# Gate logits copied out of their bank by VectorE alone, and the second half's norm factors spread by a store and a load

## Chip, cores and metric

One core of a Trainium2 chip runs the kernel. The metric is the device time of one execution in microseconds (us). The kernel before was timed in three runs; the profile shown below is of a fourth execution of the same program.

## What is computed

One layer of a decoder trunk on x of 1024 rows by 1024 columns in float32, cut here to what the change touches:

```python
h    = rms_norm(x, norm_mix_g)                  # r = (mean(x*x) + eps) ** -0.5 for each row, h = x * r * g
proj = h @ w_in                                 # q k v z_a gk_low cb cc xc z_c g_a g_c
gk   = log_sigmoid(gk_low @ w_gk2 + b_gk) / 16  # the decays, 4 heads of 128
o    = gla_chunked(q, k, v, gk)                 # uses running sums of gk in chunks of 64 rows
...
```

What is left out is the convolution branch, the gated merge, the output product, the gate of the per-layer embedding and the last norm.

## The kernel before

Everything is held transposed: columns of x on the 128 partitions, rows along the free dimension. The rows come in two halves of 512. Each large product is split into quadrants and computed by a scheme of seven products per 2x2 block (h0 to h6 are the seven combinations of h's quadrants), and each float32 operand is split into a rounded part (`hi`, made by ScalarE) and a rest (`lo`, made by VectorE), so that one product costs three matmuls (`mm3`).

The order of instructions is not the order of the program text. `Flow.note` (L270) records each operation with a cost and a latency; `set_dues` (L373) gives each a due time, counted back from the end; `put_in_order` (L420) then deals them out to the five engines' queues, one at a time: each engine takes, of the operations that are ready at the earliest moment, the one with the earliest due time. A `hurry` makes an operation due earlier by so many us. TensorE's main products (`nc.side = False`) keep the order of the text; its side products are fitted in between. `since` (L433) says from when an operation may run, by the inputs and by the release of its buffer. The queues that come out are fixed: on the chip each engine waits at the head of its queue for whatever is late.

Two places matter here.

**The norm factors, `scale_h` (L1083).** It is called for the first half of the rows (i = 0) and for the second (i = 1). For the second half ScalarE squares and sums four row blocks `xn` (128x1024), VectorE adds eps, GpSimd takes the power -0.5, which leaves `r` as 128 partitions by 4. But h needs r along the free dimension, the same on all partitions. So VectorE copies r out to `rb` (128x512), TensorE transposes four 128x128 blocks of it into a PSUM bank `rt`, and VectorE multiplies eight times: `hq <- hq * gain * rt`. From the scaled quarters `hq` VectorE and ScalarE make h1, h2, h4, h5, h6 (`step`, L1139). h0 and h3 come from the first half alone, and the eight gate products of this stage (`two_products`) use only these two.

**The decays, `decays` (L1305).** Woven into the products for v (half 0) and for z_a (half 1), a first product gives `lowp`, which is split into `low`; then for each of the four heads one matmul `zp` of 128x512 goes into a PSUM bank with the tag "o". Two such banks exist, and the main products hold one or the other of them for part of the time. The bank `zp` is read twice: ScalarE takes |zp + b| out of it into `t1`, VectorE takes min(zp + b, 0) into `c`. Exp, Ln, a subtraction and a scan along the rows follow, and a store. The pool "v" (L1273), which holds these tiles and the weights `glw` of `lowp`, takes over the memory of the pool "prep0" with the quarters `hq`.

Of the kernel before, what the change touches and what calls it, by code (L numbers as in the profile page):

```python
# [9 lines left out]
F32 = mybir.dt.float32  # L10
# [3 lines left out]
AF = mybir.ActivationFunctionType  # L14
ALU = mybir.AluOpType

P = 128
# [27 lines left out]
PE, DVE, ACT, POOL, SP = range(5)  # L45
# [197 lines left out]

class Op:
    __slots__ = ("n", "engine", "call", "args", "kw", "cost", "lat", "side", "table", "bytes", "name",
                 "preds", "succs", "left", "ready", "due", "start", "bufs", "hurry")


class Port:
# [7 lines left out]
class Flow:  # L257
# [4 lines left out]

    def __init__(self, tc):
        nc = tc.nc
        self.tc, self.ops, self.side, self.open, self.hurry, self.bundle, self.hold = tc, [], True, [], 0.0, None, None
        self.tensor, self.vector, self.scalar = Port(self, PE, nc.tensor), Port(self, DVE, nc.vector), Port(self, ACT, nc.scalar)
        self.gpsimd, self.sync = Port(self, POOL, nc.gpsimd), Port(self, SP, nc.sync)


    def note(self, engine, op, call, args, kw):  # L270
        views = [a for a in args if isinstance(a, View) or hasattr(a, "ap")]
        views += [a for k, a in kw.items() if k not in ("out", "accum_out") and (isinstance(a, View) or hasattr(a, "ap"))]
        outs, ins = ([kw["out"]], views) if "out" in kw else (views[:1], views[1:])
        if kw.get("accum_out") is not None:
            outs.append(kw["accum_out"])
        o = Op()
        o.n, o.engine, o.call, o.args, o.kw = len(self.ops), engine, call, args, kw
        o.side, o.table, o.bytes, o.bufs, o.hurry = self.side, 0, 0, [], self.hurry
        label = lambda v: v.buf.name if isinstance(v, View) else "in"
        o.name = f"{label(outs[0])}<-{','.join(label(v) for v in ins)}"  # L280
        shape = outs[0].shape
        n = 1
        for d in shape[1:]:
            n *= d
        o.lat = 0.15
        if engine == PE:
            o.cost, o.lat = n / 2400 + 0.0134, 0.22
            if op == "transpose" or args[1].dtype == F32:
                o.cost = 0.11
            elif args[1].shape[0] < P:  # L290
                o.cost = 0.42
        elif engine == DVE:
            psum = any(isinstance(v, View) and v.buf.pool.name == "ps" for v in outs + ins)
            o.cost = 0.07 + n * (0.00055 if op in ("tensor_scalar", "tensor_copy") and not psum else 0.00104)
            if op in ("scalar_tensor_tensor", "tensor_scalar"):
                o.cost += 0.06
            if op == "tensor_tensor_scan":
                o.cost = 0.05 + n * 0.0021
        elif engine == ACT:
            o.cost = 0.10 + n * 0.000833 + (0.2 if "accum_out" in kw else 0.0)  # L300
            o.table = TABLE.get(args[2] if len(args) > 2 else None, 0)
        elif engine == POOL:
            o.cost = 0.1 + n * 0.001 if op == "memset" else 0.6
        else:
            o.cost, o.bytes = 0.4, shape[0] * n * 4
            if getattr(ins[0], "apart", None):
                o.cost, o.bytes = 0.6, 1.4 * o.bytes
            o.lat = 2.0 + o.bytes / 250e3
        if op == "dma_start" and engine != SP:
            o.cost, o.lat = 0.1, 2.3 + shape[0] * n * 4 / 250e3  # L310
        preds = {}

        def behind(p):
            if p is not None and p != o.n:
                q = self.ops[p]
                lat = q.lat
                if q.engine == engine and engine != SP:
                    lat = 0.0 if engine == PE else 0.08
                preds[p] = max(preds.get(p, 0.0), lat)

        for v in ins:
            if isinstance(v, View):
                for b in v.blocks():
                    e = v.buf.memory.setdefault(b, [None, []])
                    behind(e[0])
                    e[1].append(o.n)
        for v in outs:
            if isinstance(v, View):
                for b in v.blocks():
                    e = v.buf.memory.setdefault(b, [None, []])  # L330
                    for p in [e[0]] + e[1]:
                        behind(p)
                    e[0], e[1] = o.n, []
                if engine == PE:
                    behind(v.buf.group)
                    v.buf.group = o.n
                for pool in v.buf.pool.instead:
                    for old in pool.buffers:
                        for p in old.users:
                            behind(p)  # L340
        for v in outs + ins:
            if isinstance(v, View) and v.buf not in o.bufs:
                if v.buf.index is None:
                    v.buf.index = len(v.buf.tag.buffers)
                    v.buf.tag.buffers.append(v.buf)
                o.bufs.append(v.buf)
                v.buf.users.append(o.n)
        if self.hold is not None:
            preds[self.hold] = max(preds.get(self.hold, 0.0), 0.0 if self.ops[self.hold].engine == engine else 0.08)
        o.preds, o.succs = preds, []  # L350
        for p in preds:
            self.ops[p].succs.append(o.n)
        self.ops.append(o)
        if self.bundle is not None and engine == PE:
            self.bundle.append(o)
# [64 lines left out]
    def put_in_order(self):  # L420
# [12 lines left out]
        def since(o):  # L433

            t = max(o.ready, pipe - BACKLOG) if o.engine == SP else o.ready
            for b in o.bufs:
                for e, end in b.ends.items():
                    if e != o.engine:
                        t = max(t, end + 0.13)
                if b.place is None:  # L440
                    if b.tag.next != b.index:
                        return None
                    free = min((w for w in b.tag.free if w is not None), default=None)
                    if free is None:
                        return None
                    t = max(t, free)
            return t

        while len(order) < len(ops):
# [17 lines left out]
            o = ops[n]  # L467
# [11 lines left out]
            for s in o.succs:  # L479
                q = ops[s]  # L480
# [38 lines left out]
def kernel(  # L519
# [16 lines left out]
    nc = Flow(tc)  # L536
# [29 lines left out]
    bgk = vec[:, 0:4]  # L566
# [8 lines left out]
    def dram(name, *shape):  # L575
        return dr.tile([P, *shape], F32, name=name)

    ped = [dram(f"ped{b}", D) for b in range(8)]
    s1d = [dram(f"s1d{c}", 512) for c in range(8)]
    cd = [[dram(f"cd{h}_{i}", HALF) for i in range(2)] for h in range(H)]  # L580
# [22 lines left out]
    def mm(*a, **kw):  # L603
        nc.tensor.matmul(*a, skip_group_check=True, **kw)

    def transpose(o, i):
        nc.tensor.transpose(o, i, ident)
# [433 lines left out]
    with phase("prep0") as pool:  # L1041
# [41 lines left out]
        def scale_h(i):  # L1083
# [3 lines left out]
            r = sm.tile([P, 4], F32, tag="rx", name=f"r_x{i}", bufs=2)  # L1087
            if i:
                ms = sm.tile([P, 4], F32, tag="rn", name="rn")
                for s in range(4):  # L1090
                    act(xn[s], xn[s], AF.Square, scale=1.0 / 32.0, accum_out=ms[:, s:s + 1])
                nc.vector.tensor_scalar(r, ms, EPS, None, op0=ALU.add)
            else:
                acc = slot(1, "h", "sq", (4, 512), F32)
# [8 lines left out]
                    mm(sums[:, s, 0:1], acc[:, 0, s * P:(s + 1) * P], ones, start=True, stop=True)  # L1103
                nc.vector.tensor_scalar(r, sums[:, :, 0], EPS, None, op0=ALU.add)
            nc.gpsimd.tensor_tensor(r, r, mhalf[:, 0:1].to_broadcast([P, 4]), op=ALU.pow)
            rb = bp.tile([P, 4, P], F32, tag="u2", name=f"rb{i}", bufs=2)
            nc.vector.tensor_copy(rb, r[:, :, None].to_broadcast([P, 4, P]))
            rt = pso.tile([P, 4, P], F32, tag="o", name=f"rt{i}", bufs=2)
            for s in range(4):
                transpose(rt[:, s, :], rb[:, s, :])  # L1110
            rt = rt.rearrange("p s t -> p (s t)")
            for n in both:
                for k in range(4):
                    kk = 4 * quad[n][1] + k
# [24 lines left out]
        def step(k):  # L1139
            steps[k]()  # L1140
            hres[k] = hb[k]
# [22 lines left out]
        pe_blocks(range(4, 8), 1)  # L1164
        scale_h(0)
        step(0)
        step(3)
        two_products(pre[:4], (4, 5, 0, 1))
        scale_h(1)
# [103 lines left out]
    with phase("v", [ph["prep0"]]) as qp:  # L1273
# [31 lines left out]
        def decays(half):  # L1305
# [15 lines left out]
            for hp in range(2):  # L1321
                t1 = [qp.tile([P, HALF], F32, tag="t1", name=f"t1_{half}{hp}{i}", bufs=3) for i in range(2)]
                c = [qp.tile([P, HALF], F32, tag="c4", name=f"c4_{half}{hp}{i}", bufs=4) for i in range(2)]
                for i in range(2):
                    h = 2 * hp + i
                    zp = pso.tile([P, 512], F32, tag="o", name=f"zp{half}_{h}", bufs=2)
                    cs = slice(h * P, (h + 1) * P)
                    mm(zp, g2[:, cs], low, start=True, stop=True)
                    act(t1[i], zp, AF.Abs, bias=bgk[:, h:h + 1])
                    nc.vector.tensor_scalar(c[i], zp, bgk[:, h:h + 1], 0.0, op0=ALU.add, op1=ALU.min)  # L1330
                    yield 1
                for t in t1:
                    act(t, t, AF.Exp, scale=-1.0)
# [666 lines left out]
```

## Time and profile before

| | |
|---|---|
| runs | 1078.73, 1078.83, 1078.86 us (median 1078.83) |
| profiled execution | 1078.6 us, of which the span from first to last instruction is 1076.8 us |
| TensorE (PE) busy | 1067.4 us, 99% of the span |
| weight loads (PEld) busy | 892.2 us, 83% |
| VectorE (DVE) busy | 894.3 us, 83% |
| ScalarE (ACT) busy | 623.4 us, 58% |
| GpSimd (POOL) busy | 45.7 us, 4% |
| granted TensorE clock | 0.998 |

Each row of the timeline is a start, a duration, an engine, the operation, the tiles as out<-in, the shape, and in brackets the idle time before it with what ended it. The chain of waits is the list of work that ended last, followed back from the end; its pieces are start, length and what ran. Nearly all lines carry L507, the line at which the planner issues everything, so that one goes by the names of the tiles.

### The profile page before, as it was taken

The page shows a single profiled execution, that of the slowest core. Times are in us where ns is not written, and L with a number is a line of the kernel's source. Part 1 is how long each engine was busy: PE and PEld are TensorE (multiplying, and loading weights), DVE is VectorE, ACT ScalarE, POOL GpSimd, SP SyncE. Part 2 cuts the span into 40 slices and gives each one's busy share as a digit, 9 for nine tenths or more (in the row PEclk, how much of TensorE's full clock was granted, in tenths as well). Part 3 has the DMA queues.
Part 4 walks back from the last instruction along what each step waited for, and adds up shares of the span by engine and source line. Part 5 has one row for each costly group of instructions (what it writes and reads, how often), then busy time and mean ns, then how long its engine had stood idle before and what let it go on. Part 6 is the DMA issues. An engine that isn't in the chain of part 4 may idle for free.

```text
span 1076.8 us, 15006 instructions
## 1 busy us (share of the span) xinstructions
PE 1067.4 (99%) x4989; PEld 892.2 (83%) x4989; DVE 894.3 (83%) x1409; ACT 623.4 (58%) x1141; POOL 45.7 (4%) x83
## 2 busy tenths in 40 slices
PE   9999999999999999999999999999999999999997
PEld 7887887888888888888888888888888888888886
DVE  6998567678999787978868788887999978889896
ACT  6778538656544443555444367666756635466555
POOL 0000000000000000000000011120000000011021
PEclk9999999999999999999999999999999999999999
DMA  9963564467772454554324679978586878799963
GB/s 318 368 229 105 175 209 141 152 196 234 237 222 99 140 183 166 196 194 168 127 85 126 228 238 335 325 277 332 194 305 213 286 223 305 237 337 333 313 222 140
DMA packets 144830, 239.98 MB, mean 223 GB/s; under 512 B 12016, under 2 KB 57328, under 8 KB 141808
## 3 DMA queue, kind: packets, MB, share of 16 engines
q1 hardware_dynamic: 144608, 238.76, 65.5%
q8 instruction: 39, 0.64, 0.2%
q14 instruction: 39, 0.32, 0.1%
q10 hardware_dynamic: 144, 0.26, 0.1%
HBM read 158.24 MB, written 80.74 MB: 222 GB/s over the span
## 4 chain that ended last, share of the span: by engine, by line
PE 98%; ACT 1%; DVE 0%; issue 0%; POOL 0%; ACTq 0%; DVEq 0%
PE vY L507 3%; PE zaY L507 3%; PE pe L507 2%; PE vX L507 2%; PE zaV L507 2%; PE vV L507 2%; PE op L507 2%; PE zaX L507 2%; PE kv L507 1%; PE ga1Y L507 1%; PE ga3Y L507 1%; PE xc1Y L507 1%; PE xc3Y L507 1%; PE cb2Y L507 1%; PE cb1Y L507 1%; PE xc2Y L507 1%
## 5 line engine op out<-in xcount | busy, mean ns | idle before, releaser
L507 ACT ACT_TABLE_LOAD x20 | 25.7, 1283 | 1.1 <-PEq L1989 0.7
L507 ACT ACTIVATE junk<-x 128x512 bf16<-128x512 f32 (+1 forms) x30 | 18.0, 601 | 12.2 <-DVE x L507 9.7
L507 DVE TENSOR_TENSOR wt<-wt 128x512 f32<-128x512 f32 x32 | 22.1, 691 | 0.6 <-DMA wt<-in_wb_dram 0.5
L507 DVE SCALAR_TENSOR_TENSOR u<-t,vec,u 128x1024 f32<-128x1024 f32 x16 | 20.3, 1285 | 0.1
L507 POOL MEMSET t<- 128x2 f32 x8 | 0.8, 100 | 443.2 <-PE k1Y L507 243.0
L507 POOL TENSOR_SCALAR rg<-ms 128x1 f32<-128x1 f32 x8 | 6.4, 796 | 262.5 <-ACT junk L507 262.3
L507 DVE SCALAR_TENSOR_TENSOR S<-S,dds,kv 128x256 f32<-128x256 f32 x24 | 10.5, 478 | 5.4 <-PE kv L507 5.4
L507 ACT CAST S<-S 128x512 fp32r<-128x512 f32 x14 | 8.7, 620 | 10.3 <-PE op L507 9.4
L507 ACT ACTIVATE junk<-op 128x256 bf16<-128x256 f32 x32 | 12.2, 380 | 3.0 <-PE op L507 2.9
L507 ACT ACTIVATE og<-op,or 128x256 f32<-128x256 f32 x32 | 13.3, 468 | 0.8 <-POOL or L507 0.8
L507 ACT ACTIVATE oq<-oq,vec 128x512 f32<-128x512 f32 x20 | 13.3, 716 | 0.0
L507 PE MATMUL op<-v,aTh 128*128 128x256 f32 x64 | 12.8, 283 | 0.0
L507 PE MATMUL pe<-wpehi,pTlo 128*128 128x512 f32 x32 | 12.7, 397 | 0.0
L507 PE MATMUL pe<-wpehi,pThi 128*128 128x512 f32 x32 | 12.6, 393 | 0.0
L507 PE MATMUL pe<-wpelo,pThi 128*128 128x512 f32 x32 | 12.6, 393 | 0.0
L507 DVE TENSOR_TENSOR szl<-og,szl 128x512 f32<-128x512 f32 x16 | 11.0, 687 | 1.6 <-ACT og L507 1.6
L507 POOL TENSOR_TENSOR or<-or,mhalf 128x2 f32<-128x2 f32 x16 | 11.8, 740 | 1.3
L507 DVE SCALAR_TENSOR_TENSOR hq<-hq,vec,rt 128x512 f32<-128x512 f32 x16 | 11.2, 744 | 0.6 <-PE rt L507 0.4
L507 DVE TENSOR_TENSOR x<-x,pe 128x512 f32<-128x512 f32 (+1 forms) x18 | 11.2, 632 | 0.3
L507 DVE STREAM_TRANSPOSE oT<-szl 128x512 f32<-128x512 f32 x16 | 11.3, 707 | 0.1
L507 DVE TENSOR_TENSOR u<-u,s 128x512 f32<-128x512 f32 x16 | 11.0, 690 | 0.3
L507 POOL TENSOR_SCALAR or<-oms 128x2 f32<-128x2 f32 x16 | 5.8, 363 | 124.8 <-ACT junk L507 124.8
(3183 smaller groups left out, 4203.7 us busy)
## 6 DMA issues: line engine op xcount, KB each, us to landing
wtd<-wt SPq DMA_DIRECT2D x44, 256.0 KB, 2.5
wt<-in_wb_dram SPq DMA_DIRECT2D x8, 1024.0 KB, 5.0
v<-vd SPq DMA_DIRECT2D x16, 512.0 KB, 6.2
wgq<-wtd SPq DMA_DIRECT2D x7, 1024.0 KB, 7.8
qk<-qkd SPq DMA_DIRECT2D x12, 512.0 KB, 6.0
vraw<-in_wv_dram SPq DMA_DIRECT2D x20, 256.0 KB, 4.1
zaraw<-in_wv_dram SPq DMA_DIRECT2D x20, 256.0 KB, 4.1
uq<-ud SPq DMA_DIRECT2D x5, 1024.0 KB, 7.7
```

What stands on the lines that cost most here:

```text
L507: o.call(*[place(a) for a in o.args], **{k: place(a) for k, a in o.kw.items()})
```

## The change

In `scale_h`, for the second half only, the copy to `rb` and the four transposes are gone. Instead ScalarE's queue issues a store of r to a DRAM buffer `rxd` (128x4 values, each written to its own place so that the 512 rows stand in order) and then a load that reads these 2 KB for every partition, into an SBUF tile `rt1` of 128x512. Both are due 20 us earlier than the count gives. The squares of the second half may not go ahead of the last ScalarE operation recorded before `step(3)`, the rounding of h0. The planner now keeps a latency of 1 us or more between two operations on one engine, so that the load isn't planned before the store's assumed latency has passed (2.3 us and the bytes at 250 GB/s; for the load this makes 3.35 us).

In `decays`, VectorE adds b to `zp` and writes `c`, due 6 us earlier than the count gives; ScalarE takes |c| from SBUF, and VectorE then takes min(c, 0) in place. The bank has one reader in the place of two. The matmul `zp` is planned 0.6 us later than its bank and its neighbours' releases would allow (`apart`).

```diff
@@ Flow.note
-                if q.engine == engine and engine != SP:
+                if q.engine == engine and engine != SP and lat < 1.0:
                     lat = 0.0 if engine == PE else 0.08
@@ since
+            wait = 0.13 + o.apart
...
-                        t = max(t, end + 0.13)
+                        t = max(t, end + wait)
...
-                    t = max(t, free)
+                    t = max(t, free + o.apart)
@@ scale_h
+                nc.hold = rounded[0]
                 for s in range(4):
                     act(xn[s], xn[s], AF.Square, scale=1.0 / 32.0, accum_out=ms[:, s:s + 1])
+                nc.hold = None
...
-            rb = bp.tile([P, 4, P], F32, tag="u2", name=f"rb{i}", bufs=2)
...
+            if i:
+                nc.hurry = 20.0
+                nc.scalar.dma_start(rxd.spread(0, [(1, P), (P, 4)]), r)
+                rt = bp.tile([P, 512], F32, tag="u2", name="rt1", bufs=2)
+                nc.scalar.dma_start(rt, rxd.spread(0, [(0, P), (1, 4 * P)]))
+                nc.hurry = 0.0
+            else:
+                rb = bp.tile([P, 4, P], F32, tag="u2", name=f"rb{i}", bufs=2)
...
@@ after step(0)
+        rounded = [o.n for o in nc.ops if o.engine == ACT][-1:]
@@ decays
+                    nc.apart = 0.6
                     mm(zp, g2[:, cs], low, start=True, stop=True)
-                    act(t1[i], zp, AF.Abs, bias=bgk[:, h:h + 1])
-                    nc.vector.tensor_scalar(c[i], zp, bgk[:, h:h + 1], 0.0, op0=ALU.add, op1=ALU.min)
+                    nc.apart, nc.hurry = 0.0, 6.0
+                    nc.vector.tensor_scalar(c[i], zp, bgk[:, h:h + 1], None, op0=ALU.add)
+                    nc.hurry = 0.0
+                    act(t1[i], c[i], AF.Abs)
+                    nc.vector.tensor_scalar(c[i], c[i], 0.0, None, op0=ALU.min)
```

More of the change, by code (lines that the diff above doesn't have):

```diff
@@ L245 @@
     __slots__ = ("n", "engine", "call", "args", "kw", "cost", "lat", "side", "table", "bytes", "name",
-                 "preds", "succs", "left", "ready", "due", "start", "bufs", "hurry")
+                 "preds", "succs", "left", "ready", "due", "start", "bufs", "hurry", "apart")
 class Port:
@@ L264, in __init__ @@
         nc = tc.nc
-        self.tc, self.ops, self.side, self.open, self.hurry, self.bundle, self.hold = tc, [], True, [], 0.0, None, None
+        self.tc, self.ops, self.side, self.open, self.hurry, self.bundle, self.hold, self.apart = tc, [], True, [], 0.0, None, None, 0.0
         self.tensor, self.vector, self.scalar = Port(self, PE, nc.tensor), Port(self, DVE, nc.vector), Port(self, ACT, nc.scalar)
@@ L277, in note @@
         o.n, o.engine, o.call, o.args, o.kw = len(self.ops), engine, call, args, kw
-        o.side, o.table, o.bytes, o.bufs, o.hurry = self.side, 0, 0, [], self.hurry
+        o.side, o.table, o.bytes, o.bufs, o.hurry, o.apart = self.side, 0, 0, [], self.hurry, self.apart
         label = lambda v: v.buf.name if isinstance(v, View) else "in"
@@ L576, in dram @@
         return dr.tile([P, *shape], F32, name=name)
+    rxd = dram("rxd", 4)
     ped = [dram(f"ped{b}", D) for b in range(8)]
@@ L1105, in scale_h @@
             nc.gpsimd.tensor_tensor(r, r, mhalf[:, 0:1].to_broadcast([P, 4]), op=ALU.pow)
-            rb = bp.tile([P, 4, P], F32, tag="u2", name=f"rb{i}", bufs=2)
[L1107 to L1111, printed above, removed]
+            if i:
[6 more added lines that the diff above has]
+                rb = bp.tile([P, 4, P], F32, tag="u2", name=f"rb{i}", bufs=2)
+                nc.vector.tensor_copy(rb, r[:, :, None].to_broadcast([P, 4, P]))
+                rt = pso.tile([P, 4, P], F32, tag="o", name=f"rt{i}", bufs=2)
+                for s in range(4):
+                    transpose(rt[:, s, :], rb[:, s, :])
+                rt = rt.rearrange("p s t -> p (s t)")
             for n in both:
```

## Prediction

> **What bounds the kernel now.** I read the page first, for which engine sets the time.
>
> ```profile
> span 1076.8 us, 15006 instructions
> ...
> PE 1067.4 (99%) x4989; PEld 892.2 (83%) x4989; DVE 894.3 (83%) x1409; ACT 623.4 (58%) x1141; POOL 45.7 (4%) x83
> ...
> PE 98%; ACT 1%; DVE 0%; issue 0%; POOL 0%; ACTq 0%; DVEq 0%
> ```
>
> TensorE is busy for 1067.4 of 1076.8 us and is 98% of the chain that ended last. A microsecond is won only by giving TensorE fewer matmuls or by closing one of its holes, and lost only by opening one. VectorE at 83% and ScalarE at 58% count where TensorE waits for them. The next view is therefore the list of waits of the weight loads, because a weight load that waits shows that TensorE's queue has stopped. It has ten entries in all; the five that touch the changed code are these (us in total, times, longest):
>
> ```profile
> PEld zp L507 <- ACT t L507: 0.9, 3, 0.4
> PEld zaX L507 <- ACT zax L507: 0.6, 1, 0.6
> ...
> PEld zp L507 <- DVE vlo L507: 0.4, 1, 0.4
> ...
> PEld zp L507 <- DVE c L507: 0.4, 1, 0.4
> PEld lowp L507 <- DVE vu L507: 0.3, 1, 0.3
> ```
>
> Of the five waits of `zp`, four are for a reader of `zp`'s own kind of bank: three times for ScalarE's Abs, once for VectorE's min, and the fifth is for the main product that had the bank before. What they cost TensorE is in the chain of waits, whose pieces are start, length, what.
>
> ```profile
> 41.74 0.44 PE rt L507 x4
> ...
> 51.50 2.72 PE gc0pX L507 x12
> ...
> 80.07 3.73 PE lowp L507 x16
> ...
> 89.35 0.43 PE zp L507
> ...
> 95.95 0.44 PE zp L507
> ...
> 100.50 10.88 PE vV L507 x48
> ```
>
> Twelve matmuls take 2.72 us, so one costs 0.227 us at full pace. The `zp` at 89.35 holds TensorE for 0.43 and the one at 95.95 for 0.44; one between them is like the first of these. That is 0.20, 0.20 and 0.21 us of standstill. In half 1 the timeline of TensorE shows the same at two places:
>
> ```profile
> 165.90 0.39 PE L507 MATMUL zaX<-za0hi,h0lo 128*128 128x512 f32 x1
> 166.29 0.50 PE L507 MATMUL zp<-low,g 128*128 128x512 f32 x1
> 166.62 0.40 PE L507 MATMUL zaX<-za0hi,h0hi 128*128 128x512 f32 x1
> ...
> 170.07 0.39 PE L507 MATMUL zaX<-za0hi,h0lo 128*128 128x512 f32 x1
> 170.61 0.50 PE L507 MATMUL zaX<-za3hi,h3hi 128*128 128x512 f32 x1 [0.15 <-ACT zax L507]
> 170.95 0.39 PE L507 MATMUL zaX<-za3lo,h3hi 128*128 128x512 f32 x1
> ```
>
> The starts, not the durations, are to be compared. From 165.90 to 166.62 two matmuls take 0.72 us where 0.45 is the pace: 0.27 lost at `zp`. From 170.07 to 170.95 they take 0.88: 0.43 lost, this time at a main product that waits for ScalarE's copy `zax`.
>
> **The change, part by part.** The **four transposes** of `rt` go: 0.44 us of TensorE (the row at 41.74), with no cover to lose, so the term is -0.44.
>
> The **zp matmuls** have one reader fewer in their bank, the one left is due 6 us earlier, and each is planned 0.6 us later than its release. What stood still was 0.20 to 0.27 us each, less than this margin, and main products stand ready in TensorE's queue to fill it. I take all four as closed: -0.20 - 0.20 - 0.21 - 0.27 = -0.88. The bounds are 0 (the margin is used up by a VectorE that runs later than planned) and -0.88.
>
> The **hole at 170.6** is not named in the change. ScalarE is late there by this:
>
> ```profile
> 168.16 1.28 ACT L507 ACT_TABLE_LOAD   x1
> ```
>
> The load serves the Exp of the first head, put ahead of `zax`. With Abs behind VectorE's addition, Exp comes later, and the planner may deal the table load behind `zax` or not. The bounds are 0 and -0.43; I take half, -0.2.
>
> **VectorE and ScalarE in the decays.** VectorE gets eight more operations (min in SBUF). The nearest row is a tensor_scalar in SBUF of twice the width:
>
> ```profile
> L507 DVE TENSOR_SCALAR u<-t,vec 128x1024 f32<-128x1024 f32 x8 | 6.0, 751 | 0.0
> ```
> ```profile
> 82.00:100.00 18.00, 18.00 (x77) 13.96 (x76) 15.33 (x24) 14.89 (x23) 0.00 (x0) 1.00 0.16 55
> 160.00:180.00 20.00, 19.84 (x86) 15.59 (x85) 17.02 (x27) 15.41 (x24) 0.00 (x0) 1.00 0.51 173
> ```
>
> Half the width lies between half of 0.751 and all of it, 0.38 to 0.75 us; nearer the half, since the row copies no bank, so 0.4 us and 1.6 us a half. The third figure behind the bar of each stretch (after TensorE and the weight loads) is VectorE's busy time: it idles for 2.67 of 18.00 us in the first half's stretch and 2.98 of 20.00 in the second's. 1.6 us fits into both, and the idle is what covers it; without that cover it would be up to 3.0 us a half (four times 0.75). The min also waits for Abs on ScalarE, and behind it on VectorE's queue stand the `lo` splits of the weights. The bound is one ScalarE operation of lateness for each min; none of it is TensorE's as long as those splits run ahead of their products, as they do in before, where no wait of these weights is among the five rows above. I take 0, with 0 to +1 for the range.
>
> **The store and the load of r** replace a path on which the first scaled quarter began at 42.21, 1.8 us after r was there:
>
> ```profile
> 39.39 1.02 POOL L507 TENSOR_TENSOR r_x<-r_x,mhalf 128x4 f32<-128x4 f32 x1 [16.80 <-DVE r_x L507]
> ```
> ```profile
> 42.21 1.41 DVE L507 SCALAR_TENSOR_TENSOR hq<-hq,vec,rt 128x512 f32<-128x512 f32 x2
> ...
> 77.44 0.50 DVE L507 TENSOR_TENSOR glw<-graw,glw 128x128 fp32r<-128x128 f32 x2
> ```
> ```profile
> s1d<-ga2ps SPq DMA_DIRECT2D x1, 256.0 KB, 7.1
> ```
> ```profile
> L507 ACTq DMA_DIRECT2D out_dram<-x x1: 406/406/406, 1073.1 to 1073.1; - x1
> ```
> ```profile
> out_dram<-x ACTq DMA_DIRECT2D x1, 256.0 KB, 2.7
> ```
> ```profile
> 40.00:60.00 20.00, 20.00 (x92) 16.57 (x91) 19.72 (x26) 15.31 (x23) 0.41 (x1) 1.00 0.94 337
> ```
>
> No transfer of so small a kind, and none on ScalarE's queue at this time, is in the trace. The nearest are a transfer of 256 KB on ScalarE's queue at the end of the kernel, on idle engines, 2.7 us from issue to landing, and one on SyncE's queue at 40 us, 7.1 us, behind a full queue. The DMA engines are 94% busy here. Each of the two transfers is therefore 2.7 to 7.1 us. I take 4.0 including the issue: nearer to 2.7, since nothing else stands in ScalarE's queue, and above it, since the engines are shared. r is there at 40.41, so `rt1` lands at 48.4 (45.8 to 54.6), 6.2 us after the old start.
>
> Who waits for that? On VectorE the quarters and all that comes of them, and the planner knows of most: its own latencies (2.31 and 3.35 and two issues of 0.1) give 5.86 us, and it fills VectorE's queue with the splits of the gate weights meanwhile. What is late against the plan is 8.0 - 5.86 = 2.1 us. On ScalarE the load waits at the head of the queue until the store has landed, and the roundings behind it with it:
>
> ```profile
> 44.91 1.05 ACT L507 CAST h4hi<-hq 128x1024 fp32r<-128x1024 f32 x1 [2.57 <-DVE hq L507]
> ```
>
> ScalarE idled for 2.57 us at this place before, so a wait of that size is covered, and the two issues of 0.41 us each with it. TensorE has work from h0 and h3 alone until `lowp` at 80.07, which needs `glw`, made at 77.94 in memory that the quarters must have left. That is 2.1 us of spare, just the lateness that I reckon, and the next user, the product of h1 (`vV`, at 100.50), is 20 us further on. So the term is 0, and if the spare is gone TensorE loses us for us. On the other side, r's squares are due some 4 us earlier and r may be there sooner; a gain for TensorE does not come of it, as nothing waits for h1 today. The copy `rb` and the bank `rt` that VectorE no longer touches lie on the same covered stretch and count 0.
>
> Here the Trainium skill speaks against the change: "DMA: Bandwidth & Descriptors", section Rules for kernel authors, says that a last dimension without contiguous runs costs one descriptor per element, and its Specifications say that pieces below 512 bytes are read, modified and written. The store of r is 512 pieces of 4 bytes. That page of the Trainium skill has no time for such a store; by it the store would lie towards the upper bound. The same page of the Trainium skill, section Queues, rings and completion order, has each DMA engine take turns between the queues, so that a transfer on ScalarE's queue would not stand behind SyncE's backlog; by that both would lie towards the lower bound. No run here shows either yet.
>
> The **sum** is -0.44 - 0.88 - 0.2 + 0 + 0 = -1.5 us. On the profiled execution (span 1076.8, 1078.6 with what lies around it) that makes 1077.1; the median of the runs shown, 1078.83, lies 0.2 above that execution, so the forecast is 1077.3. A measurement of this kernel tells some 0.2%, 2.16 us, from no change; this gain is 0.14%.
>
> **Rivals.** *R1, the path of r is late and TensorE stops at `lowp`: slower.* At the upper bounds store and load take 14.2 us with two issues of 0.41, 15.0 in all, 9.1 more than the planner's 5.86. Less the 2.1 us of spare, TensorE loses 7.0, the sum is +5.5 and the time 1084.3. It decides the sign at a stop of 1.5 us (a path of 9.5 us), and it makes the kernel slower by over 2.16 us from a stop of 3.7 us, a path of 11.7 us. For it: saturated engines, a queue that stops at its head, and a VectorE busy for 19.72 of 20 us at 40 to 60, which has no room to catch up. Against it: both transfers would have to be as slow as those behind a full queue. The Trainium skill's rule on small pieces is on its side.
>
> *R2, the stalls move but stay.* The planner's guesses for VectorE and ScalarE have missed by 0.2 to 0.4 us at each `zp`; eight more operations on VectorE can eat the margin of 0.6, and other holes can open as the whole order is dealt anew. Then only the transposes are won: -0.44, give or take 0.5, 1078.4.
>
> *R3, all holes close: faster.* -0.44 - 0.88 - 0.43, and the 0.3 at `lowp` too, is -2.05 or 1076.8. For a verdict of faster a further 0.1 us is needed, from the new deal of the rest; 1076.6 is about the floor, as TensorE's other waits lie outside the changed code.
>
> *R4, the change does nothing,* because the planner's new order puts `zp` late enough to delay the product behind it (`vV` needs the same two banks): the 0.6 us margins then come back as one hole of up to 1 us at 100.50, and the time is 1078.3.
>
> **How the numbers follow.** My sum has a chance of 0.45, R2 and R4 together 0.19, R1 0.19, R3 0.17. R1 gives most of slower: 0.15 of it beyond 2.16 us and 0.04 short of that; new holes elsewhere in R2's deal add 0.04 to slower. R3 lies on the edge: I count 0.15 as faster. So faster 0.15, slower 0.19, within 0.2% 0.66. The range goes from R3's floor, 1076.6, to 1080.6, where R1 has a stop of some 3.3 us; what is left out is R1's worse part and a tail below the floor.
>
> **What would show it.** In the changed profile: no `rt` for the second half, and PE's pieces of `zp` at 0.23 us, with the waits of PEld for `t` and `c` gone. `rt1` should land 5 to 9 us after r, the first scaled quarter start at 45 to 50, and `lowp` have no wait over 0.3 us. `zax` with a hole of 0 or 0.43 settles the half that I took. The prediction is wrong if PEld waits for `glw` or for a weight split of v or z_a, if the path of r takes over 11.7 us, or if new waits appear behind 200 us, where nothing was changed but the order.

## The result, and the profile after

| | before | after |
|---|---|---|
| median of four runs each, same chip | 1078.78 us (1078.64 to 1078.86) | 1092.50 us (1090.19 to 1094.09) |
| profiled execution | 1078.6 us, span 1076.8 | 1092.08 us, span 1090.3 |
| granted TensorE clock, mean | 0.998 | 0.992 |

The change makes the kernel slower: the ratio is 1.0125 with a 95% interval of 1.0113 to 1.0137. The forecast was 1077.3 and the range ended at 1080.6. The span grew by 13.5 us, and that is what has to be found. First the page of the profile after:

```profile
span 1090.3 us, 15011 instructions
...
PE 1070.7 (98%) x4985; PEld 896.0 (82%) x4985; DVE 896.4 (82%) x1416; ACT 624.1 (57%) x1143; POOL 45.6 (4%) x83
...
PE 95%; DMA 2%; DVE 1%; ACT 1%; issue 0%; SPq 0%; POOL 0%; ACTq 0%; DVEq 0%
```

TensorE's share of the chain of waits fell from 98 to 95%, and 2% of it, which was none before, is a DMA. TensorE is also busy for 3.3 us more with four matmuls fewer. So there are two things to look for: time in which it stands, and time in which it runs slower. The waits of the weight loads name the first (us in total, times, longest):

```profile
PEld gc0pX L508 <- ACT pe L508: 8.2, 1, 8.2
PEld gc0pX L508 <- ACT gc0ps L508: 2.8, 1, 2.8
```

The five waits of `zp` and the one of `zaX` are gone from the list, and the one of `lowp` is 0.3 as before. The two that are new are both at `gc0pX`, the first product of the second four gate products, which I had counted among the work that TensorE can do meanwhile. Why it could not is seen in the timelines of GpSimd (first row) and ScalarE; the last row is of ScalarE in before:

```profile
38.49 1.02 POOL L508 TENSOR_TENSOR r_x<-r_x,mhalf 128x4 f32<-128x4 f32 x1 [15.64 <-DVE r_x L508]
...
42.15 0.38 ACTq L508 DMA_DIRECT2D rxd<-r_x  x1
42.58 0.62 ACT L508 CAST gc1phi<-gc1praw 128x512 fp32r<-128x512 f32 x1 [2.86 <-DMA gc0praw<-in_wc_dram]
...
58.10 0.34 ACTq L508 DMA_DIRECT2D rt<-rxd  x1
58.48 0.58 ACT L508 COPY pe<-pe 128x512 f32<-128x512 f32 x1 [14.28 <-DMA rxd<-r_x]
```
```profile
41.23 0.59 ACT L507 COPY pe<-pe 128x512 f32<-128x512 f32 x1
```

r is there at 39.51, but the store goes out only at 42.15. The chain of waits shows what it waited for:

```profile
35.33 6.75 DMA hq<-in_xT_dram
...
42.15 15.87 DMA rxd<-r_x
```

It is a load of `hq` from SyncE's queue, whose data the store does not need; in the instructions as built, the two count on the same semaphore. Then the load of `rt1` stands at the head, 14.28 us long, until the store has landed. Behind the load is the copy of a `pe` block out of PSUM. That block lies in bank 2, the bank that `two_products(pre[4:], (2, 3, 4, 5))` gives to `gc0pX`. In before the same copy ran at 41.23. So TensorE waited for a bank, and the bank for a copy that had nothing to do with r except its place in a queue.

The transfers themselves (issues in the stretch from 40 to 62 us: queue, size, us from issue to landing; the last row is of before):

```profile
gc1praw<-in_wc_dram SPq DMA_DIRECT2D x1, 256.0 KB, 14.8
...
rt<-rxd ACTq DMA_DIRECT2D x1, 256.0 KB, 3.2
rxd<-r_x ACTq DMA_DIRECT2D x1, 2.0 KB, 15.9
```
```profile
gc1praw<-in_wc_dram SPq DMA_DIRECT2D x1, 256.0 KB, 7.1
```

The store of 2 KB took 15.9 us, the load of 256 KB behind it 3.2. And the weights of the gate products, on another queue, took twice as long as before. The windows show what moved (stretch, length, busy TensorE, weight loads, VectorE, ScalarE, GpSimd, granted clock, DMA share, GB/s; the third row is of before):

```profile
42.00:58.00 16.00, 9.30 (x42) 7.35 (x40) 1.38 (x2) 1.62 (x3) 0.00 (x0) 0.90 1.07 188
58.00:66.00 8.00, 6.88 (x18) 5.45 (x19) 5.34 (x9) 3.60 (x5) 0.00 (x0) 0.57 0.46 156
```
```profile
42.00:58.00 16.00, 16.00 (x73) 13.24 (x72) 15.82 (x21) 11.41 (x16) 0.00 (x0) 1.00 0.93 331
```

The DMA engines show as fully busy (share 1.07) while they move 188 GB/s instead of 331. VectorE and ScalarE work for 1.4 and 1.6 us of 16. And in the eight microseconds after the stop the granted clock is 0.57. The last is the second loss. The timeline of TensorE, of which only the starts count:

```profile
50.91 0.39 PE L508 MATMUL ga3pX<-h3hi,ga3plo 128*128 128x512 f32 x1
59.12 0.79 PE L508 MATMUL gc0pX<-h0hi,gc0phi 128*128 128x512 f32 x1 [7.82 <-ACT pe L508]
...
65.12 0.40 PE L508 MATMUL gc1pX<-h0hi,gc1plo 128*128 128x512 f32 x1
...
72.61 0.39 PE L508 MATMUL gc3pX<-h0hi,gc3plo 128*128 128x512 f32 x1
75.40 0.80 PE L508 MATMUL gc0pX<-h3hi,gc0phi 128*128 128x512 f32 x1 [2.40 <-ACT gc0ps L508]
...
78.82 0.40 PE L508 MATMUL gc0pX<-h3hi,gc0plo 128*128 128x512 f32 x1
```

At the pace of 0.227 us, TensorE stands for 59.12 - 50.91 - 0.23 = 7.98 and for 75.40 - 72.61 - 0.23 = 2.56 us. From 59.12 to 65.12 are 14 matmuls in 6.00 us where the pace makes 3.18, which loses 2.82; from 75.40 to 78.82 are 8 in 3.42, which loses 1.60. Together 14.96. Against it stand the four transposes (-0.44) and the holes at `zp` and `zaX` (-1.31), which makes +13.2 of the 13.5. The last 0.3 lies at the start of the kernel, ahead of all changed code: the fifth `pe` matmul starts at 7.05 in the place of 6.75, because the four before it ran slower. What made them slower isn't shown.

The second stop hangs on the first quarter of h:

```profile
61.35 0.75 DVE L508 SCALAR_TENSOR_TENSOR hq<-hq,vec,rt 128x512 f32<-128x512 f32 x1 [1.04 <-DMA rt<-rxd]
...
66.66 1.05 ACT L508 CAST h6hi<-hq 128x1024 fp32r<-128x1024 f32 x1 [4.54 <-DVE hq L508]
```

It begins at 61.35 where it was 42.21. ScalarE then stands for 4.54 us before the rounding of h6, and the copy `gc0ps`, for which `gc0pX` waits a second time, comes behind that.

### The profile page after: what moved, and what is told of

Same layout as the page of the kernel before. It is cut to its first block, busy times and chain, and to the rows that moved or that the text cites. A ratio compares the mean times of both kernels' runs of the same rounds, so it can differ in the third digit from the quotient of the medians.

```text
span 1090.3 us, 15011 instructions
## 1 busy us (share of the span) xinstructions
PE 1070.7 (98%) x4985; PEld 896.0 (82%) x4985; DVE 896.4 (82%) x1416; ACT 624.1 (57%) x1143; POOL 45.6 (4%) x83
## 4 chain that ended last, share of the span: by engine, by line
PE 95%; DMA 2%; DVE 1%; ACT 1%; issue 0%; SPq 0%; POOL 0%; ACTq 0%; DVEq 0%
PE vY L508 3%; PE zaY L508 3%; PE vX L508 2%; PE zaX L508 2%; PE zaV L508 2%; PE vV L508 2%; PE op L508 2%; PE pe L508 2%; DMA rxd<-r_x 1%; PE kv L508 1%; PE gc0pX L508 1%; PE ga1Y L508 1%; PE ga3Y L508 1%; PE cb2Y L508 1%; PE xc2Y L508 1%; PE xc3Y L508 1%
## 5 line engine op out<-in xcount | busy, mean ns | idle before, releaser
L508 ACT COPY pe<-pe 128x512 f32<-128x512 f32 x8 | 4.6, 581 | 16.7 <-DMA rxd<-r_x 14.3
L508 ACT ACTIVATE oq<-oq,vec 128x512 f32<-128x512 f32 x20 | 13.2, 715 | 0.0
L508 DVE SCALAR_TENSOR_TENSOR hq<-hq,vec,rt 128x512 f32<-128x512 f32 x16 | 11.2, 744 | 1.5 <-DMA rt<-rxd 1.0
L508 POOL TENSOR_TENSOR or<-or,mhalf 128x2 f32<-128x2 f32 x16 | 11.8, 738 | 1.3
L508 DVE TENSOR_TENSOR x<-x,pe 128x512 f32<-128x512 f32 (+1 forms) x18 | 11.2, 630 | 0.3
```

Of the source, the lines that this page charges most:

```text
L508: o.call(*[place(a) for a in o.args], **{k: place(a) for k, a in o.kw.items()})
```

## The experiments

**The two halves of the change apart.** The first kernel has the decays of the changed kernel and the transposes of the kernel before; the second the reverse.

```diff
# decays only, against after (scale_h)
-                nc.hold = rounded[0]
...
-            if i:
-                ... store, rt1, load ...
-            else:
+            rb = ...; nc.vector.tensor_copy(rb, ...); four transposes into rt
```

> The decays' part alone, r's second half by the copy and the transposes as before. If the loss comes from the path of r alone: the holes at zp and at zaX close as in the changed kernel, 0.9 to 1.4 us faster than before, 1077.4 to 1077.9. If the new order of the decays has a share in the loss: slower than before, 1080 or more.

Measured: 1077.51 us (1077.05 to 1078.02) beside 1079.02 for before on the same chip, ratio 0.9987 (0.9978 to 0.9996), span 1075.5. The chain of waits has all four `zp` of the first half at full pace, and the timeline of ScalarE shows the table load behind the copies `zax`:

```profile
86.84 0.23 PE zp L508
...
94.45 0.23 PE zp L508
```
```profile
170.16 0.58 ACT L508 COPY zax<-zaX 128x512 f32<-128x512 f32 x1
170.76 1.28 ACT L508 ACT_TABLE_LOAD   x1
```

The decays do what they are meant to do: the holes at `zp` and the one at `zaX` are all closed, and the span is 1.3 us shorter, as 0.88 + 0.43 makes. Which of the three means closed those at `zp` (one reader fewer, the earlier due time, the 0.6 us) isn't shown, as this run has all three.

> The store and the load of r alone, the decays as before. If the path of r makes the whole loss, the gain of the decays is missing and all else is there: some 15 us slower than before, 1092 to 1095, with the store landing after 12 to 18 us. If the loss needs both parts: 1079 to 1086.

Measured: 1093.97 us (1092.19 to 1094.98), ratio 1.0138 (1.0124 to 1.0152). Its weight loads wait at the same two places:

```profile
PEld gc0pX L508 <- ACT pe L508: 9.7, 1, 9.7
PEld gc0pX L508 <- ACT gc0ps L508: 4.2, 1, 4.2
```

So the whole loss comes with the path of r. That half also keeps the squares behind the rounding of h0 (`hold`), which no run takes apart from the store and the load.

**The store, without anyone who waits for it.** To the kernel of the decays only a store of r is added that nothing reads; the transposes stay. In one kernel it is the store of the change, 512 pieces of 4 bytes; in the other the same 2 KB leave as 128 pieces of 16 bytes.

```diff
+            if i:
+                nc.hurry = 20.0
+                nc.scalar.dma_start(rxd.spread(0, [(1, P), (P, 4)]), r)    # e3: 512 x 4 bytes
+                nc.scalar.dma_start(rxd.spread(0, [(4, P), (1, 4)]), r)    # e9: 128 x 16 bytes
+                nc.hurry = 0.0
```

> e1 with the store of r added on ScalarE's queue, which nothing reads; the transposes stay, so that nobody waits for the store to land but later transfers that share its semaphore. If the loss is ScalarE standing at the load until the store has landed: within 1 us of e1, 1077 to 1079, although the store still takes over 10 us. If the loss is the slowing of all other transfers beside the 4-byte pieces: 1082 to 1090, with the loads issued at 40 to 46 us landing after 12 to 15 us as in the changed kernel.

> This is the kernel of the decays' part alone (1077.5 us) with a store of r that nothing reads, as in the run of the unread store, but written as 128 pieces of 16 bytes in the place of 512 of 4. Theory (the pieces of 4 bytes slow their neighbours, and that is what cost 3.7 us there): the store lands after 5 to 8 us in the place of 15.5, the loads of 256 KB issued beside it (gc1praw, gc2praw, gc3praw, s1d) take 5 to 8.5 us as in before and not 12 to 15, TensorE has no wait at gc0pX over 1 us, and the time is 1077 to 1079. Rival (any store put into ScalarE's queue at this place costs this much, by its issue and by the order that it brings): the hole at gc0pX stays, and the time is 1080 to 1083.

Measured: 1081.18 us (1078.45 to 1082.50, ten runs), ratio 1.0016 (1.0007 to 1.0025), with the small pieces, and 1077.38 us (1076.87 to 1078.11, eleven runs), ratio 0.9988 (0.9979 to 0.9996), with the larger. The issues from 40 to 62 us, a wait of the weight loads and one of ScalarE with the small pieces, then the issues with the larger:

```profile
gc1praw<-in_wc_dram SPq DMA_DIRECT2D x1, 256.0 KB, 11.3
...
rxd<-r_x ACTq DMA_DIRECT2D x1, 2.0 KB, 15.5
```
```profile
PEld gc0pX L508 <- ACT gc0ps L508: 2.5, 1, 2.5
```
```profile
58.27 0.69 ACT L508 ACTIVATE g<-ga2pX,vec 128x512 f32<-128x512 f32 x1 [4.19 <-DMA s1d<-ga3ps]
```
```profile
gc1praw<-in_wc_dram SPq DMA_DIRECT2D x1, 256.0 KB, 8.0
...
rxd<-r_x ACTq DMA_DIRECT2D x1, 2.0 KB, 5.8
```

A store that nobody reads costs 1081.18 - 1077.51 = 3.7 us over the decays alone when it has 512 pieces, and nothing that can be seen when it has 128 (1077.38 against 1077.51). Its place in ScalarE's queue and its 2 KB are the same, and its issue takes 0.40 and 0.34 us. The cost is therefore in the number and size of the pieces, which change together here. It reaches TensorE through the other transfers: `gc1praw` and its three neighbours take 11 to 14 us, ScalarE stands for 4.19 us until one of them, the store `s1d<-ga3ps`, has landed, its copy `gc0ps` comes late, and one stop of 2.25 us with slow matmuls behind it opens. The 3.7 us are the middle of a wide spread, and the median lies between the two times that were expected; the trace is of a run of 1081.71. With the larger pieces the theory holds in every point that was named.

**The path of r with larger pieces.** The first of these stores 16 bytes of each partition and lets VectorE read `rt1` in strides of 16 bytes. The second turns r by one transpose first and stores four pieces of 512 bytes; the load is the old one.

```diff
# e4, against after
-                nc.scalar.dma_start(rxd.spread(0, [(1, P), (P, 4)]), r)
+                nc.scalar.dma_start(rxd.spread(0, [(4, P), (1, 4)]), r)
...
+                    rk = rt.rearrange("p (t s) -> p s t", s=4)       # second half only
# e6, against after
...
+                transpose(rp[0:4, :], r)
...
+                nc.vector.tensor_copy(rr[0:4, :], rp[0:4, :])
-                nc.scalar.dma_start(rxd.spread(0, [(1, P), (P, 4)]), r)
+                nc.scalar.dma_start(rxd.spread(0, [(P, 4), (1, P)]), rr[0:4, :])
```

> The changed kernel with r stored as it lies, 128 pieces of 16 bytes, and the order of rows taken up by the reader's stride. If it is the number of small pieces that makes the store slow: it lands after 4 to 8 us and the time is 1077 to 1082. If it is the queue or the busy engines whatever the pieces: 12 us or more, and 1088 to 1094.

> The changed kernel with r turned by one small transpose first, so that the store is 4 pieces of 512 bytes. If small pieces make the store slow and slow down the others: it lands after 2 to 4 us, the loads beside it after 6 to 8 us as in before, and the time is 1078 to 1084, the rest of the loss being the path that is still longer than planned. If the way through DRAM at this busy time is itself the cause: 1086 or more.

Measured: 1087.08 us (1086.37 to 1088.08), ratio 1.0076 (1.0063 to 1.0090), and 1083.01 us (1082.23 to 1084.12), ratio 1.0039 (1.0024 to 1.0054). In the first the store takes 6.4 us, as expected, the load behind it 4.0, and the transfers beside it 6 to 8.6; the time is 5 us above the expected range all the same. The reading in strides costs VectorE something else. The group of its multiplies, of after and of this run (mean ns of one behind the comma; half of the 16 are of the first half of the rows and unchanged):

```profile
L508 DVE SCALAR_TENSOR_TENSOR hq<-hq,vec,rt 128x512 f32<-128x512 f32 x16 | 11.2, 744 | 1.5 <-DMA rt<-rxd 1.0
```
```profile
L508 DVE SCALAR_TENSOR_TENSOR hq<-hq,vec,rt 128x512 f32<-128x512 f32 x16 | 14.2, 933 | 2.3 <-DMA rt<-rxd 1.9
```

Eight multiplies at 2 x 0.933 - 0.744 = 1.12 us instead of 0.74 make 3.0 us more on an engine that has no room at this place, and TensorE's stops add up to 7.6 us. How much of the 7.6 hangs on the strides isn't shown. The Trainium skill, "SBUF — State Buffer", section Door 1: The DMA port swizzle, says that SBUF is read in lines of 16 bytes and that each step to a new line pays; with one value used of each line, this run agrees.

In the second, the slowdown of the neighbours and the strides are both gone, and TensorE has one stop left. The timelines of ScalarE and VectorE:

```profile
48.05 0.36 ACTq L508 DMA_DIRECT2D rt<-rxd  x1
48.45 0.62 ACT L508 CAST gc3phi<-gc3praw 128x512 fp32r<-128x512 f32 x1 [3.89 <-DMA gc1praw<-in_wc_dram]
```
```profile
53.45 2.74 DVE L508 SCALAR_TENSOR_TENSOR hq<-hq,vec,rt 128x512 f32<-128x512 f32 x4 [3.05 <-DMA rt<-rxd]
```

The first quarter still comes at 53.45, 11.2 us later than in before, and TensorE stops for 3.6 us at `gc0pX` with some eight slow matmuls behind it. That is what is left of the loss with this store. But the store isn't all that holds this path up. It goes out at 42.90, again behind a transfer on its semaphore. The load behind it goes out at 48.05, and what ended last before it was not the store but `gc1praw`, a load of weights issued at 40.92 that landed 7.1 us later, at 48.03; in the instructions as built it counts on the same semaphore as the load of `rt1`. The view has no landing time for this store, so how long it took itself isn't known.

**Telling the planner.** Perhaps the wait costs so much only because the planner counts 2.31 us for the store. In two runs its latencies were raised: to 19 us for the store of after, and to 5.0 and 5.6 us for the store and load of the kernel with r turned first.

```diff
+            if label(outs[0]) == "rxd":
+                o.lat = 19.0                                   # e5; 5.0 in e10
+            if label(outs[0]).startswith("rt1"):
+                o.lat = 5.6                                    # e10 only
```

> The changed kernel with one number of the planner changed: it counts 19 us for the store of r instead of 2.3. If the loss is the queue standing for a transfer that the plan took for short: ScalarE has the load much later in its queue and doesn't stand at it for over 3 us, and the time is that of the unread store, 1079 to 1083. If the quarters come too late however the queue is dealt: TensorE stops at a later place and the time stays over 1087.

> The kernel with one transpose of r first and a store of four pieces of 512 bytes (1083.0 us), and the planner counts 5.0 us for the store and 5.6 us for the load, as measured there, in the place of 2.3 and 3.35. Theory (what was left there was the difference between a path counted as 5.9 us and one of some 12, on which the queues of ScalarE and VectorE stood): ScalarE doesn't stand at the load, the hole of 3.9 us at gc0pX goes below 1.5 us, and the time is 1078 to 1081. Rival (the quarters are too late for the order however it is dealt, as with the planner told of a store of 19 us): other holes open for those that close, and the time stays at 1082 to 1086.

Measured: 1093.28 us (1092.99 to 1094.14), ratio 1.0134 (1.0118 to 1.0151), and 1084.27 us (1082.72 to 1084.82), ratio 1.0052 (1.0037 to 1.0068). Neither is better than its kernel with the old latencies, 1092.50 and 1083.01: the times are those of the rival in both. ScalarE no longer stands for 14 us at the load in the first, and the stop at `gc0pX` is gone in both. But the weight loads wait elsewhere (three rows of each, then ScalarE behind the load in the second):

```profile
PEld gc2pX L510 <- ACT gc2ps L510: 3.1, 1, 3.1
PEld vX L510 <- DVE v0lo L510: 3.0, 1, 3.0
...
PEld vV L510 <- DVE c L510: 1.7, 1, 1.7
```
```profile
PEld zp L512 <- DVE c L512: 2.0, 1, 2.0
PEld vV L512 <- DVE c L512: 1.7, 1, 1.7
...
PEld vX L512 <- DVE v0lo L512: 1.3, 1, 1.3
```
```profile
47.77 0.62 ACT L512 CAST gc0phi<-gc0praw 128x512 fp32r<-128x512 f32 x1 [4.07 <-DMA s1d<-ga2ps]
```

What TensorE waits for now is for the most part the work of VectorE: splits of v's weights, and the readers of `zp` (the copy `gc2ps` is ScalarE's). VectorE had been busy for 15.82 of the 16 us from 42 to 58 in before. I read this so: work that is put off for 11 us and more has no free place afterwards, and another order only chooses which of TensorE's products pays. Neither run is a clean test of it. In the first the store landed at 47.7, after 11.8 us, but the load was dealt for a store of 19 us and went out at 59.05. In the second ScalarE still stands for 4.07 us at the load, until `s1d<-ga2ps` has landed, another transfer that only shares the load's semaphore; and the 5.0 us counted for the store are that kind of wait too, not a measurement of the store.

**Another queue.** Store and load are issued by GpSimd instead of ScalarE, so that nothing stands behind the load in ScalarE's queue.

```diff
-                nc.scalar.dma_start(rxd.spread(0, [(1, P), (P, 4)]), r)
+                nc.gpsimd.dma_start(rxd.spread(0, [(1, P), (P, 4)]), r)
...
-                nc.scalar.dma_start(rt, rxd.spread(0, [(0, P), (1, 4 * P)]))
+                nc.gpsimd.dma_start(rt, rxd.spread(0, [(0, P), (1, 4 * P)]))
```

> The changed kernel with the store and the load issued from GpSimd's queue instead of ScalarE's. If ScalarE standing at the load makes most of the loss: ScalarE no longer stands, VectorE stands at the first quarter instead, and the time falls to 1081 to 1087. If the late quarters on VectorE's queue cost as much: 1088 to 1094.

Measured: 1091.77 us (1090.89 to 1092.70), ratio 1.0119 (1.0104 to 1.0135). The waits, us in total, times, longest:

```profile
DVE hq L508 <- DMA rt<-rxd: 18.0, 1, 18.0
...
PEld gc1pX L508 <- DVE pe L508: 9.1, 1, 9.1
```

The stand is now at the head of VectorE's queue, and behind it is the other `pe` copy, the one of bank 3, which `gc1pX` needs. The stop has moved on by one product and is no shorter, 8.8 us where it was 8.0. The store took 14.6 us from this queue as well, so its duration isn't a matter of ScalarE's queue. It also went out at 39.98, 0.3 us after r, with no wait for the load of `hq`, and `rt1` landed at 61.4 as in the changed kernel, since the load took 6.2 us in the place of 3.2.

**The slow matmuls.** To the kernel with the unread store of small pieces, twelve matmuls are added whose result nothing reads, ahead of the second round of the gate products, so that TensorE doesn't stop there.

```diff
...
+                fill = pso.tile([P, 512], F32, tag="o", name="fill", bufs=2)
...
+                for n in range(12):
+                    mm(fill, hres[0][0][:, 0, 0:P], hres[0][0][:, 0, :], start=True, stop=True)
```

> The kernel with the unread store and twelve matmuls more, which nothing reads, put where TensorE stopped for 2.3 us before the second products of the gate group. If a stop of that length makes the matmuls after it slow (0.427 us in place of 0.227): the hole is filled, the matmuls after it run at 0.227, and the time is some 1 to 2 us below the unread store's, 1079 to 1080. If the slow matmuls have another cause: they stay, and the time is the unread store's or more, 1081 to 1084.

Measured: 1083.25 us (1081.55 to 1084.72), ratio 1.0040 (1.0025 to 1.0055). The stop at `gc0pX` and the matmuls at 0.427 us are gone from the trace, but the twelve matmuls cost 2.7 us themselves, the order was dealt anew, and there is one stop that none of the others has (1.67 us of standstill by the starts of the matmuls around it):

```profile
PEld lowp L508 <- issue: 1.9, 1, 1.9
```

So the trace shows no slow matmul where there is no long stop. It is of a run of 1081.83; two of the four took 1084.7, and the time decides nothing.

## Why the prediction was wrong

**The four transposes** were priced rightly at -0.44: 0.30 us behind the kernel before at 7 us, TensorE is 0.18 ahead of it just after their place (the same `ga0pX` matmul starts at 42.07 in the place of 42.25). That the work put in their place was free is what failed.

**The `zp` matmuls** came out at the -0.88 that I took. **The hole at `zaX`** was taken at half, -0.2, and closed whole, -0.43, because the table load was dealt behind the copies (170.76 in the run of the decays alone). **VectorE's eight operations** were estimated at 0.4 us each and cost nothing on the path; their group in the profile after:

```profile
L508 DVE TENSOR_SCALAR c<-c 128x512 f32<-128x512 f32 x8 | 3.3, 421 | 0.0
```

The decays alone give -1.3 us in the spans and -1.5 in the medians, where their part of the sum was -1.1. That part stands, and no kernel that was run is faster than the one with it alone beyond noise; the one with the unread store of 16-byte pieces is level.

**The store and the load of r** were taken at 0 on TensorE and cost 15 us. Five steps of that part failed.

The first is the price of the store. I bounded it by transfers of whole rows, 2.7 to 7.1 us; it took 15.9, and 11.8 to 16.6 in the other kernels that issue it. My rows said how long contiguous runs take on idle and on full engines; none of them could say what 512 pieces cost, and I kept their upper end as the upper end of the unknown. Of the two rules that I set against each other, the one on small pieces had the direction right: the Trainium skill, "DMA: Bandwidth & Descriptors", section Rules for kernel authors, and its Specifications. 128 pieces of 16 bytes took 5.8 us at the same place. The other rule of the Trainium skill, the turns between the queues, did not help: the store was slow on either queue.

The second is its effect on others. I priced the store as a thing that is slow or quick by itself. It doubled the time of SyncE's transfers, and the unread store shows that this alone is worth 3.7 us in the medians.

The third is the start. I let the path begin when r was there. The store was issued 2.64 us later, behind the load of `hq`. The path came to 21.8 us, from 39.51 to 61.30, where I had 8.0 and, in R1, 15.0 at most; 11.7 was the sign of being wrong that I had named. By itself this step doesn't decide: from GpSimd's queue the store went out at once, and the loss was much the same.

The fourth is the cover, and it is the step that decides. I counted ScalarE's idle time of 2.57 us at this place as the cover of a wait, and took `lowp`, 40 us on, as the first place where TensorE would stop. I looked for who needs h1 and its like, the data that depend on r. Who stood there was a copy that doesn't depend on r but lay behind the load in the same queue and held bank 2. I had written that the roundings behind the load wait with it, and didn't ask which banks and weights those instructions set free. TensorE's cover ended at 51.13, with the last matmul that needed nothing of ScalarE.

The fifth is the pace after a stop: 4.4 of the 15 us are matmuls at 0.427 us, for which my sum had no term.

**The rivals.** R1 was right in kind: the path late, a queue that stops at its head, VectorE without room to catch up. Its rule, the path less 5.86 less 2.1, makes 13.8 with the measured 21.8 us, and the measured loss is 15.0. That the two are near is partly chance, as R1 has TensorE stop at `lowp` and knows nothing of slow matmuls. Its end, 1084.3, was too low, because its upper bound stood on the wrong rows, and its weight of 0.19 leaned on the same rows. R3's mechanism came true in the decays. R2's and R4's didn't: no new hole opened at `zp` or at `vV` in the changed kernel.

What remains open is whether a path of r through DRAM can be had at no cost here. The best one that was tried, 512-byte pieces with the first quarter at 53.45, is 5.5 us behind the kernel with four transposes. The shortest path that was measured, with the store of 16 bytes, is 13.6 us from r to the landing of `rt1`; one of 8 us was not reached. In all three kernels that read `rt1` from a store of larger pieces, the load of `rt1` went out when an unrelated transfer on its semaphore landed. A path with larger pieces and semaphores of its own was not run, so how much of the 5.5 us is that wait stays open.

## What to carry to other kernels

Before an instruction that waits for a transfer is put into an engine's queue, go through what stands behind it in that queue and ask of each which bank, buffer or weight it sets free for TensorE; the first of these, not the first user of the transferred data, is the end of the cover. Count the pieces of a small store, not its bytes, look up which earlier transfers its issue has to wait for, and let no transfer of long rows stand as the upper bound of a scattered one. Four short transposes on the engine that bounds the kernel can be cheaper than a detour that is free on paper.

## What the runs showed of the hardware

A store of 2 KB in 512 pieces of 4 bytes took 11.8 to 16.6 us beside loads of weights on another queue, whose own time went from 7.1 to 14.8 us (`gc1praw`, before and after); the engines showed as fully busy at 188 GB/s. In 128 pieces of 16 bytes it took 5.8 to 6.4 us, and the transfers beside it stayed at 5 to 8.6 us.

A DMA's issue waited for an earlier transfer that had nothing to do with it but the semaphore on which both count, as built: the store of r until 42.08 for a load of `hq` (the changed kernel), the load of `rt1` until 48.03 for `gc1praw` (r turned first).

After a stop TensorE ran at a granted clock of 0.57 in the stretch and started its matmuls every 0.427 us instead of 0.227, for some microseconds. In all the runs, each single stop of 2.25 us or more had such matmuls behind it, and no single stop of up to 1.88 us had. The Trainium skill, "TensorE: Matmul & The Clock Gate", section Part 1: The HAM clock gate, has the clock halved after an idle window of about 3.4 us that runs freely; the pace agrees, but here 2.25 us of standstill were enough. Two stops close together gave no clear answer: 0.77 and 1.63 us with one matmul between had slow ones behind them, 1.75 and 1.64 us with one between had none.
